# Decay table of a gated delta rule: differences and mask on GpSimd, one exponential per 16 rows and direction

## The chip, the cores and the metric

The kernel runs on one core of a Trainium2 chip. The metric is the device time of one execution in microseconds; the median of the runs counts. The engines are TensorE (PE in the profile, its weight loads PEld), VectorE (DVE), ScalarE (ACT), GpSimd (POOL) and SyncE (SP, which issues loads). Each engine works through its own instructions in a fixed order; semaphores tie the engines together.

## The reference, cut to what matters

One encoder layer over 512 tokens (two sequences of 256), width 2048: an RMS norm, one input projection, eight heads of neighbourhood attention beside eight heads of a gated delta rule that runs in both directions, an output projection, a SwiGLU, and a last norm. The change concerns the delta rule. Its per-token decay `g` is summed along each chunk of 64 tokens, and each pair of tokens of a chunk gets the decay between them:

```python
g = jnp.cumsum(g.reshape(B, n, CHUNK, H).transpose(0, 3, 1, 2), axis=-1)
tri = jnp.tril(jnp.ones((CHUNK, CHUNK), dtype=bool))
diff = g[..., :, None] - g[..., None, :]
decay = jnp.where(tri, jnp.exp(jnp.where(tri, diff, 0.0)), 0.0)
a_mat = jnp.where(strict, jnp.einsum('bhncd,bhnsd->bhncs', k_beta, k) * decay, 0.0)
qk = jnp.where(tri, jnp.einsum('bhncd,bhnsd->bhncs', q, k) * decay, 0.0)
```

`a_mat` is then inverted (a triangular solve), and a recurrence over the four chunks follows.

## The kernel before

A "lane" is one chunk of one head, sequence and direction: 4 x 8 x 2 x 2 = 128 lanes, one per partition. Lanes 0 to 63 (`half[0]`) run forwards, 64 to 127 (`half[1]`) backwards. The table of decays is `E`, 64 x 64 values per lane: `E[lane, s, c] = exp(G[c] - G[s])` for c >= s forwards and c <= s backwards, zero elsewhere. `G` is the running sum of `g`.

The projection is a long list of column tiles (`col_tile`): each is two halves (`half_gemm`), a half being 24 matmuls of 128x512 (three products of high and low parts for each of eight slices). The weights of a half are loaded by SP (`w_raw`) and split into `w_hi` (ACT, L139) and `w_lo` (DVE, L140); there are three buffers of each, so a half is split while PE works on one of the two before it. TensorE's order is pinned. Between matmuls `pump()` advances generators that put side work into the same queues.

First come the eight delta-rule heads: per head a k and a q tile. Each is scaled out of PSUM (`ev_xi`, DVE L308), convolved with five taps (`cacc`: one ACT instruction at L352, four DVE instructions at L358), and put through Silu (`kq`, ACT L362). The q tile is squared and split (`q_sq` L611, `sqh`, `sql`). `gates()` computes the gates and `G` beside head 0 (L456, L457). From head `DECAY_HEAD` = 2 on, `decays` adds that head's share of the exponentials right after `sqh` and `sql`, and their place in ACT's order is pinned. Some tiles later `kq_post` runs for the head: 16 small matmuls into two `ps_s` tiles (the Gram products), a third `ps_s` tile for sums of squares; ACT copies them out (`gs` L386, `qrow` L394), and GpSimd stores them (`s_gram` L388, `s_qq` L395; `s_kq` L623). The pool `psm` has three `ps_s` tiles in all, and `gs` has one buffer for each of the two sequences.

After head 7's Gram products are stored, `lanes()` begins: GpSimd loads all of them as `kkq` (L497), ACT copies the table to the other half of the partitions (L502), DVE multiplies it by `E` (L548, L556, L557), and then runs the triangular solve column by column (`prod` L578, `W` L580), beside the neighbourhood attention's projection (`qT` L709, `kT` L714). The recurrence, the output projection and the SwiGLU follow.

A scheduler orders the instructions of DVE, ACT and GpSimd by its own estimate of when they are ready, except where the source pins them.

Of the kernel before, what the change touches and what calls it, by code (L numbers as in the profile page):

```python
# [8 lines left out]
F32 = mybir.dt.float32  # L9
# [3 lines left out]
AF = mybir.ActivationFunctionType  # L13
ALU = mybir.AluOpType
# [4 lines left out]
P = 128  # L19
# [6 lines left out]
C = 64  # L26
# [38 lines left out]

ROW_FACTORS = 24
DECAY_HEAD = 2
DECAY_ROWS = 11


def r32(ap):
# [4 lines left out]
def hybrid_encoder(ctx: ExitStack, tc: tile.TileContext, xT, w_in, w_ba, w_out, w_gate,  # L76
                   w_up, w_down, w_group, nw_mix, nw_ffn, nw_fin, na_bias, conv_w, lane_par,
                   dn_nw, y):
    nc = tc.nc
    act = nc.scalar.activation  # L80
    tt = nc.vector.tensor_tensor
    ts = nc.vector.tensor_scalar
    stt = nc.vector.scalar_tensor_tensor

    pin = tc.keep_in_program_order
# [50 lines left out]
    def split(hi, lo, src, scale=None):  # L136

        if scale is None:
            act(out=hi, in_=src, func=AF.Copy)  # L139
            tt(lo, src, r32(hi), ALU.subtract)  # L140
        else:
            act(out=hi, in_=src, func=AF.Copy, scale=scale)
            stt(lo, src, scale, r32(hi), ALU.mult, ALU.subtract)
# [31 lines left out]
    def advance(queue):  # L175
        while queue:
            try:
                next(queue[0])
                return
            except StopIteration:  # L180
                queue.pop(0)
# [19 lines left out]
    def pause(n):  # L201
        for _ in range(n):
            yield
# [11 lines left out]
    def col_tile(src, xs):  # L215
        ps = pg.tile([P, T], F32, tag="g", name="ps_g")
        half_gemm(ps, src[0], xs[:8], True, False)
        half_gemm(ps, src[1], xs[8:], False, True)
        return ps
# [121 lines left out]
    half = (slice(0, 64), slice(64, 128))  # L341
# [6 lines left out]
    def conv_silu(ps, ct, out):  # L348

        xi = evac(ps, "xi", 2)  # L350
        ac = wk.tile([P, T], F32, tag="cacc", bufs=1, name="cacc")
        act(out=ac, in_=xi, func=AF.Copy, scale=cw[:, ct, 2:3])  # L352
        x3 = xi.rearrange("p (b t) -> p b t", b=NB)
        a3 = ac.rearrange("p (b t) -> p b t", b=NB)
        for j in (0, 1, 3, 4):
            o = j - 2
            lo, hi = max(0, -o), L - max(0, o)
            stt(a3[:, :, lo:hi], x3[:, :, lo + o:hi + o], cw[:, ct, j:j + 1], a3[:, :, lo:hi],  # L358
                ALU.mult, ALU.add)
        o5 = out.rearrange("p (b q c t) -> p b q c t", b=NB, q=2, c=2)  # L360
        for pp in range(2):
            pin(act(out=o5[:, :, pp], in_=ranged(ac, pp), func=AF.Silu))  # L362
# [39 lines left out]
    ln = ln_cm.__enter__()  # L402
# [7 lines left out]
    def vec(nm, w=C):  # L410
        return ln.tile([P, w], F32, tag=nm, name=nm)

    gt = {}

    def gates():
        bl, al = vec("bl", 4 * C), vec("al", 4 * C)
        for d in range(2):
            for t, r in ((bl, d * 8), (al, 16 + d * 8)):
                for k in range(4):
                    p0 = d * 64 + k * 16  # L420
                    nc.gpsimd.dma_start(
                        t[p0:p0 + 16].rearrange("p (g t) -> p g t", g=4),
                        s_ba[:, r:r + 8].rearrange("g h (b c t) -> (h b) g c t", b=NB, c=4)[:, :, k])
        yield from pause(GATE_START)
        for t in (bl, al):
            pin(tt(t[:, :2 * C], t[:, :2 * C], t[:, 2 * C:], ALU.add))
            pin(tt(t[:, :C], t[:, :C], t[:, C:2 * C], ALU.add))
        bl, al = bl[:, :C], al[:, :C]

        xa, ax, e, z, z2, sp = vec("xa"), vec("ax"), vec("e"), vec("z"), vec("z2"), vec("sp")  # L430
        pin(ts(xa, al, lpar[:, 0:1], None, ALU.add))
        act(out=ax, in_=xa, func=AF.Abs)
        act(out=e, in_=ax, func=AF.Exp, scale=-1.0)
        ea = vec("ea", 1)
        act(out=ea, in_=lpar[:, 1:2], func=AF.Exp)
        yield
        pin(ts(z, e, 2.0, None, ALU.add))
        pin(nc.vector.reciprocal(z, z))
        pin(tt(z, z, e, ALU.mult))
        pin(tt(z2, z, z, ALU.mult))  # L440
        pin(ts(sp, z2, 1.0 / 17, 1.0 / 15, ALU.mult, ALU.add))
        for n in (13, 11, 9, 7, 5, 3, 1):
            if n % 4 == 1:
                yield
            pin(tt(sp, sp, z2, ALU.mult))
            pin(ts(sp, sp, 1.0 / n, None, ALU.add))
        yield
        pin(stt(sp, sp, 2.0, z, ALU.mult, ALU.mult))
        pin(stt(sp, xa, 0.0, sp, ALU.max, ALU.add))
        g = vec("g")  # L450
        pin(ts(g, sp, ea, -1.0, ALU.mult, ALU.mult))

        on = vec("on")
        nc.vector.memset(on, 1.0)
        G, NG = vec("G"), vec("NG")
        nc.vector.tensor_tensor_scan(G[half[0]], on[half[0]], g[half[0]], 0.0, ALU.mult, ALU.add)  # L456
        nc.vector.tensor_tensor_scan(G[half[1], ::-1], on[half[1]], g[half[1], ::-1], 0.0,  # L457
                                     ALU.mult, ALU.add)
        ts(NG, G, -1.0, None, ALU.mult)
        tot = vec("tot", 1)  # L460
        nc.vector.tensor_copy(tot[half[0]], G[half[0], C - 1:C])
        nc.vector.tensor_copy(tot[half[1]], G[half[1], 0:1])

        yield
        beta = vec("beta")
        act(out=beta, in_=bl, func=AF.Exp, scale=-1.0)
        ts(beta, beta, 1.0, None, ALU.add)
        nc.vector.reciprocal(beta, beta)

        kd, eg, el = vec("kd", 2 * C), vec("eg"), vec("el", 1)  # L470
        act(out=kd[:, :C], in_=G, func=AF.Exp, scale=-1.0, bias=tot)
        act(out=eg, in_=G, func=AF.Exp)
        act(out=el, in_=tot, func=AF.Exp)
        nc.vector.tensor_copy(kd[:, C:], kd[:, :C])
        dg = vec("dg", P)
        ts(dg, ident, el, None, ALU.mult)
        E = ln.tile([P, C, C], F32, tag="E", name="E")
        nc.gpsimd.memset(E, 0.0)
        gt.update(G=G, NG=NG, beta=beta, kd=kd, eg=eg, dg=dg, E=E)

    def decays(s0, s1):

        G, NG, E = gt["G"], gt["NG"], gt["E"]
        for s in range(s0, s1):
            pin(act(out=E[half[0], s, s:], in_=G[half[0], s:], func=AF.Exp,  # L485
                    bias=NG[half[0], s:s + 1]))
            pin(act(out=E[half[1], s, :s + 1], in_=G[half[1], :s + 1], func=AF.Exp,  # L487
                    bias=NG[half[1], s:s + 1]))

    def lanes():  # L490
        beta, kd, eg, dg, E = (gt[n] for n in ("beta", "kd", "eg", "dg", "E"))
# [112 lines left out]
    for h in range(H):  # L604
        kq = wk.tile([P, 2, T], F32, tag="kq", bufs=2, name="kq")
        ps = (ps_k0, ps_k1)[h] if h < 2 else col_tile(w_in[2 * h], xs)
        conv_silu(ps, 8 + h, kq[:, 0])
        ps = (ps_q0, ps_q1)[h] if h < 2 else col_tile(w_in[2 * h + 1], xs)
        conv_silu(ps, h, kq[:, 1])
        sq = na.tile([P, T], F32, tag="qT", name="q_sq")  # L610
        pin(act(out=sq, in_=kq[:, 1], func=AF.Square))  # L611
        sqh = na.tile([P, T], F32R, tag="s0", name="sqh")
        sql = na.tile([P, T], F32R, tag="s1", name="sql")
        split(sqh, sql, sq)
        if h == 0:
            side.append(gates())
            advance(side)
        if h >= DECAY_HEAD:
            while side:
                advance(side)  # L620
            s0 = (h - DECAY_HEAD) * DECAY_ROWS
            decays(s0, min(C, s0 + DECAY_ROWS))
        nc.gpsimd.dma_start(s_kq[h], kq)  # L623
        chains.append(kq_post(h, kq, sqh, sql))

# [812 lines left out]
```

## Time and profile before

| | |
|---|---|
| median of 3 runs | 2275.26 us (2273.75 to 2276.0) |
| the profiled execution's own time | 2273.82 us |
| its span | 2272.0 us |
| busy: PE, DVE, ACT, POOL | 99%, 78%, 47%, 10% |
| granted TensorE clock | 0.998 |
| delta-rule heads | about 0 to 216 us |
| start of `lanes()` to the end of its solve | about 223 to 480 us |

The span runs from the first instruction of the program to the end of the last. Busy PE says that matmuls are in flight, not that they flow at their best; what TensorE waited for, and when, is in the waits by engine. In a timeline, a row is one instruction or several merged ones (x2), with its start, its time, and in brackets the idle time of the engine before it and what ended that.

### The profile page before, as it was taken

Reading aid. Unit: us, or ns where it says so; the run is one execution under the profiler, and the core shown is the slowest. Engines: PE = TensorE matmul, PEld = TensorE weight load, DVE = VectorE, ACT = ScalarE, POOL = GpSimd, SP = SyncE. Lnnn points to the kernel's source line nnn. Section 1 sums busy time; section 2 is a strip of 40 time slices with the busy share of each in tenths; the row PEclk is TensorE's granted clock in tenths of the full one; section 3 lists DMA queues with packets and bytes.
Section 4 is the critical chain, followed back from the end, with each engine's and each line's share of the span. In section 5 each row is a group of like instructions: output and inputs, shape, how many; then the busy total and the mean of one; then the engine's idle time right before and its main releaser. Section 6 shows DMA issues by size and latency. Waiting matters only on the chain.

```text
span 2272.0 us, 32550 instructions
## 1 busy us (share of the span) xinstructions
PE 2242.9 (99%) x12306; PEld 1918.1 (84%) x12306; DVE 1765.7 (78%) x2713; ACT 1065.2 (47%) x1670; POOL 236.9 (10%) x343
## 2 busy tenths in 40 slices
PE   9999999999999999999999999999999999999998
PEld 7787778888888888888888888888888878888887
DVE  7754699974556546898888888888888788998966
ACT  6777332333433425644444444444444454444435
POOL 1221100010000010110111110101100011011010
PEclk9999999999999999999999999999999999999999
DMA  5343422354333555777777777777777477667672
GB/s 212 113 137 133 122 94 96 103 132 143 103 103 103 186 176 172 218 200 206 203 198 203 193 206 203 212 200 205 201 198 190 148 201 202 174 190 210 183 201 87
DMA packets 113117, 383.96 MB, mean 169 GB/s; under 512 B 14112, under 2 KB 14448, under 8 KB 112704
## 3 DMA queue, kind: packets, MB, share of 16 engines
q1 hardware_dynamic: 77552, 267.17, 34.6%
q0 software_dynamic: 34256, 112.61, 23.5%
q8 instruction: 97, 1.59, 0.3%
q10 hardware_dynamic: 1152, 2.10, 0.3%
q14 instruction: 60, 0.49, 0.1%
HBM read 346.41 MB, written 35.41 MB: 168 GB/s over the span
## 4 chain that ended last, share of the span: by engine, by line
PE 83%; DVE 7%; ACT 5%; DMA 3%; issue 2%; SPq 0%; POOL 0%; DVEq 0%; ACTq 0%; POOLq 0%
PE ps_g L88 27%; PE ps_d L88 14%; PE ps_c L88 14%; PE ps_a L88 14%; PE ps_b L88 7%; PE ps_s L88 6%; DVE w_lo L140 2%; DVE cacc L358 1%; ACT w_hi L139 1%; DVE prod L578 1%; DMA w_first<-in_w_group_dram 1%; DMA w_raw<-in_w_in_dram 1%; ACT E L485 1%; DVE W L580 1%; ACT E L487 1%
## 5 line engine op out<-in xcount | busy, mean ns | idle before, releaser
L88 PE MATMUL ps_g<-xhi,w_hi 128*128 128x512 f32 x880 | 352.2, 400 | 1.0 <-ACT w_hi L139 1.0
L88 PE MATMUL ps_g<-xhi,w_lo 128*128 128x512 f32 x880 | 344.5, 392 | 2.1 <-DVE w_lo L140 2.0
L88 PE MATMUL ps_g<-xlo,w_hi 128*128 128x512 f32 x880 | 343.6, 391 | 0.5 <-DVE xlo L258 0.5
L140 DVE TENSOR_TENSOR w_lo<-w_raw,w_hi 128x1024 fp32r<-128x1024 f32 x164 | 200.2, 1221 | 140.4 <-ACT w_hi L139 138.7
L139 ACT ACTIVATE w_hi<-b 128x1024 fp32r<-128x1024 f32 (+1 forms) x180 | 185.8, 1032 | 237.0 <-issue 119.4
L139 ACT ACTIVATE w_hi<-w_raw 128x1024 fp32r<-128x1024 f32 x164 | 172.6, 1057 | 241.9 <-PE ps_g L88 188.8
L139 ACT ACTIVATE w_hi<-w_first 128x1024 fp32r<-128x1024 f32 (+1 forms) x180 | 185.4, 1030 | 185.9 <-PE ps_c L88 90.2
L140 DVE TENSOR_TENSOR w_lo<-w_first,w_hi 128x1024 fp32r<-128x1024 f32 (+1 forms) x180 | 213.7, 1187 | 65.2 <-ACT w_hi L139 61.7
L140 DVE TENSOR_TENSOR w_lo<-b,w_hi 128x1024 fp32r<-128x1024 f32 (+1 forms) x180 | 213.0, 1183 | 7.5 <-ACT w_hi L139 7.0
L88 PEld LDWEIGHTS ps_g<-xhi,w_lo 128*128 128x128 f32 x880 | 165.3, 188 | 40.0 <-DVE w_lo L140 4.8
L88 PEld LDWEIGHTS ps_g<-xhi,w_hi 128*128 128x128 f32 x880 | 165.5, 188 | 37.1 <-issue 2.6
L88 PEld LDWEIGHTS ps_g<-xlo,w_hi 128*128 128x128 f32 x880 | 165.6, 188 | 33.5 <-DVE xlo L258 1.2
L88 PE MATMUL ps_d<-xc,w_hi 128*128 128x512 f32 x704 | 175.2, 391 | 0.0
L88 PE MATMUL ps_c<-xc,w_hi 128*128 128x512 f32 x704 | 175.2, 391 | 0.0
L88 PE MATMUL ps_a<-xc,w_hi 128*128 128x512 f32 x696 | 173.1, 391 | 0.0
L88 PEld LDWEIGHTS ps_c<-xc,w_hi 128*128 128x128 f32 x704 | 129.5, 188 | 24.9
L88 PEld LDWEIGHTS ps_d<-xc,w_hi 128*128 128x128 f32 x704 | 129.4, 188 | 24.9
L88 PEld LDWEIGHTS ps_a<-xc,w_hi 128*128 128x128 f32 x696 | 128.1, 188 | 24.7
L139 ACT ACTIVATE w_hi<-w_second 128x1024 fp32r<-128x1024 f32 (+1 forms) x60 | 62.0, 1034 | 97.9 <-DVE ga L1134 45.0
L88 PE MATMUL ps_d<-xc,w_lo 128*128 128x256 f32 x704 | 98.6, 283 | 0.0
L88 PE MATMUL ps_c<-xc,w_lo 128*128 128x256 f32 x704 | 98.6, 283 | 0.0
L88 PE MATMUL ps_a<-xc,w_lo 128*128 128x256 f32 x696 | 97.5, 283 | 0.0
(381 smaller groups left out, 4231.9 us busy)
## 6 DMA issues: line engine op xcount, KB each, us to landing
w_raw<-in_w_in_dram SPq DMA_DIRECT2D x108, 512.0 KB, 3.3
b<-in_w_gate_dram SPq DMA_DIRECT2D x66, 512.0 KB, 4.2
b<-in_w_up_dram SPq DMA_DIRECT2D x66, 512.0 KB, 4.9
b<-in_w_group_dram SPq DMA_DIRECT2D x48, 448.0 KB, 4.1
w_raw<-in_w_out_dram SPq DMA_DIRECT2D x32, 512.0 KB, 3.4
w_raw<-in_w_down_dram SPq DMA_DIRECT2D x24, 512.0 KB, 4.0
w_second<-in_w_gate_dram SPq DMA_DIRECT2D x22, 512.0 KB, 7.0
w_first<-in_w_gate_dram SPq DMA_DIRECT2D x22, 512.0 KB, 4.5
```

The costliest lines, as they stand in the source:

```text
L88: pin(nc.tensor.matmul(*a, **k))
L139: act(out=hi, in_=src, func=AF.Copy)
L140: tt(lo, src, r32(hi), ALU.subtract)
L358: stt(a3[:, :, lo:hi], x3[:, :, lo + o:hi + o], cw[:, ct, j:j + 1], a3[:, :, lo:hi], ALU.mult, ALU.add)
L485: pin(act(out=E[half[0], s, s:], in_=G[half[0], s:], func=AF.Exp, bias=NG[half[0], s:s + 1]))
L487: pin(act(out=E[half[1], s, :s + 1], in_=G[half[1], :s + 1], func=AF.Exp, bias=NG[half[1], s:s + 1]))
L578: stt(pv, W[:, s0:s1, s0:c], ndm[:, c:c + 1], kkq[:, c, 0, None, s0:c].broadcast_to([P, n, j]), ALU.mult, ALU.mult)
L580: nc.vector.tensor_reduce(W[:, s0:s1, c], pv, AX.X, ALU.add)
```

## The change

`decays` no longer issues one exponential per row s and direction, 22 rows-and-directions per head over six heads. It works on 16 rows at a time (`Q` = 16), for heads 2 to 5 only. For each of the two directions GpSimd subtracts `G[s]` from `G[c]` for the 16 rows and all columns from the block's first (forwards) or up to its last (backwards): 16 x 64, 48, 32 or 16 values per lane, straight into `E`. A third GpSimd instruction adds `far` to the 16 x 16 block on the diagonal; `far` holds 0 in the triangle that is wanted and -1e30 in the other, so that the exponential gives zero there. Then one exponential per direction works on the whole block in place. `far` is written once, in `gates()`, by 31 memsets on GpSimd. The negated sum `NG` is gone.

```diff
-DECAY_ROWS = 11
+Q = 16
...
-        ts(NG, G, -1.0, None, ALU.mult)
...
+        far = ln.tile([P, Q, Q], F32, tag="far", name="far")
+        nc.gpsimd.memset(far, 0.0)
+        for s in range(Q):
+            if s:
+                nc.gpsimd.memset(far[half[0], s, :s], -1e30)
+            if s < Q - 1:
+                nc.gpsimd.memset(far[half[1], s, s + 1:], -1e30)
...
-    def decays(s0, s1):
-        G, NG, E = gt["G"], gt["NG"], gt["E"]
-        for s in range(s0, s1):
-            pin(act(out=E[half[0], s, s:], in_=G[half[0], s:], func=AF.Exp,
-                    bias=NG[half[0], s:s + 1]))
-            pin(act(out=E[half[1], s, :s + 1], in_=G[half[1], :s + 1], func=AF.Exp,
-                    bias=NG[half[1], s:s + 1]))
+    def decays(q):
+        G, E, far = gt["G"], gt["E"], gt["far"]
+        sl = slice(q * Q, q * Q + Q)
+        blocks = [E[half[0], sl, q * Q:], E[half[1], sl, :q * Q + Q]]
+        for hf, to in enumerate((G[half[0], q * Q:], G[half[1], :q * Q + Q])):
+            shape = [C, Q, to.shape[1]]
+            nc.gpsimd.tensor_tensor(blocks[hf], to[:, None].broadcast_to(shape),
+                                    G[half[hf], sl, None].broadcast_to(shape), op=ALU.subtract)
+        nc.gpsimd.tensor_tensor(E[:, sl, sl], E[:, sl, sl], far, op=ALU.add)
+        for b in blocks:
+            pin(act(out=b, in_=b, func=AF.Exp))
...
-        if h >= DECAY_HEAD:
+        if 0 <= h - DECAY_HEAD < C // Q:
             while side:
                 advance(side)
-            s0 = (h - DECAY_HEAD) * DECAY_ROWS
-            decays(s0, min(C, s0 + DECAY_ROWS))
+            decays(h - DECAY_HEAD)
```

TensorE's instructions and their order are the same. Three places show how the others move.

First ScalarE, from the end of head 2's exponentials on. Before, the last four of the 22 and what follows them:

```order
L485 ACTIVATE E<-G,NG 64x55
L487 ACTIVATE E<-G,NG 64x10
L485 ACTIVATE E<-G,NG 64x54
L487 ACTIVATE E<-G,NG 64x11
L362 ACT_TABLE_LOAD
L362 ACTIVATE kq<-cacc 128x2x128 x2
L386 COPY gs<-ps_s 128x256 x2
L394 COPY qrow<-ps_s 1x2x2x64
L394 COPY qrow<-ps_s 1x2x128
L139 ACTIVATE w_hi<-w_raw 128x1024
```

And now, from head 2's `sqh` on:

```order
L139 ACTIVATE sqh<-q_sq 128x512
L498 ACT_TABLE_LOAD
L498 ACTIVATE E<-E 64x1024
L498 ACTIVATE E<-E 64x16x16
L386 COPY gs<-ps_s 128x256
L139 ACTIVATE w_hi<-w_raw 128x1024
L362 ACT_TABLE_LOAD
L362 ACTIVATE kq<-cacc 128x2x128 x2
L386 COPY gs<-ps_s 128x256
L394 COPY qrow<-ps_s 1x2x2x64
L394 COPY qrow<-ps_s 1x2x128
```

Two exponentials stand where 22 stood. Of head 1's two `gs` copies the first now comes right behind them, the second behind a weight split and head 3's Silu of k (`kq`), which needs DVE's convolution.

Second GpSimd, from the stores of head 0's Gram products on. Before:

```order
L623 DMA s_kq<-kq 128x1024 x2
L388 DMA s_gram<-gs 64x2x128 x4
L395 DMA s_qq<-qrow 2x4x64
L623 DMA s_kq<-kq 128x1024
L388 DMA s_gram<-gs 64x2x128 x4
L395 DMA s_qq<-qrow 2x4x64
```

And now the same stretch, as far as the second quarter's mask:

```order
L632 DMA s_kq<-kq 128x1024 x2
L388 DMA s_gram<-gs 64x2x128 x2
L494 TENSOR_TENSOR E<-G 64x1024
L494 TENSOR_TENSOR E<-G 64x16x16
L388 DMA s_gram<-gs 64x2x128
L496 TENSOR_TENSOR E<-E,far 128x16x16
L388 DMA s_gram<-gs 64x2x128
L494 TENSOR_TENSOR E<-G 64x16x48
L395 DMA s_qq<-qrow 2x4x64
L494 TENSOR_TENSOR E<-G 64x16x32 x2
L496 TENSOR_TENSOR E<-E,far 128x16x16
```

All twelve subtractions and masks, those of heads 3 to 5 too, stand here in one run; head 2's `s_kq` and the stores of head 1 come behind the last of them.

Third ScalarE again, from head 7's `sqh` to the copies of `kkq`. Before, the last exponentials and what follows:

```order
L485 ACTIVATE E<-G,NG 64x1
L487 ACTIVATE E<-G,NG 64x64
L139 ACTIVATE w_hi<-w_raw 128x1024
L386 COPY gs<-ps_s 128x256 x2
L394 COPY qrow<-ps_s 1x2x2x64
L394 COPY qrow<-ps_s 1x2x128
L139 ACTIVATE w_hi<-w_raw 128x1024 x2
L502 COPY kkq<-kkq 64x2048 x2
```

And now:

```order
L139 ACTIVATE sqh<-q_sq 128x512
L139 ACTIVATE w_hi<-w_raw 128x1024
L386 COPY gs<-ps_s 128x256 x2
L394 COPY qrow<-ps_s 1x2x2x64
L394 COPY qrow<-ps_s 1x2x128
L139 ACTIVATE w_hi<-w_raw 128x1024 x2
L512 COPY kkq<-kkq 64x2048 x2
```

Head 7's `gs` copies no longer stand behind that head's share of exponentials (18 of them).

More of the change, by code (lines that the diff above doesn't have):

```diff
@@ L454, in gates @@
         nc.vector.memset(on, 1.0)
-        G, NG = vec("G"), vec("NG")
+        G = vec("G")
         nc.vector.tensor_tensor_scan(G[half[0]], on[half[0]], g[half[0]], 0.0, ALU.mult, ALU.add)
@@ L478, in gates @@
         nc.gpsimd.memset(E, 0.0)
-        gt.update(G=G, NG=NG, beta=beta, kd=kd, eg=eg, dg=dg, E=E)
-    def decays(s0, s1):
-        G, NG, E = gt["G"], gt["NG"], gt["E"]
-        for s in range(s0, s1):
-            pin(act(out=E[half[0], s, s:], in_=G[half[0], s:], func=AF.Exp,
-                    bias=NG[half[0], s:s + 1]))
-            pin(act(out=E[half[1], s, :s + 1], in_=G[half[1], :s + 1], func=AF.Exp,
-                    bias=NG[half[1], s:s + 1]))
+        far = ln.tile([P, Q, Q], F32, tag="far", name="far")
[5 more added lines that the diff above has]
+                nc.gpsimd.memset(far[half[1], s, s + 1:], -1e30)
+        gt.update(G=G, far=far, beta=beta, kd=kd, eg=eg, dg=dg, E=E)
+    def decays(q):
[9 more added lines that the diff above has]
+            pin(act(out=b, in_=b, func=AF.Exp))
     def lanes():
```

## The prediction

> **What bounds the kernel now.** The page's first part names the engine, the waits of TensorE say what it waited for in the stretch that the change can reach (80 to 300 us), and the windows cut that stretch into pieces.
>
> ```profile
> PE 2242.9 (99%) x12306; PEld 1918.1 (84%) x12306; DVE 1765.7 (78%) x2713; ACT 1065.2 (47%) x1670; POOL 236.9 (10%) x343
> ```
>
> ```profile
> engine line waited for: us in total, times, longest us
> PE ps_s L88 <- DVE kT L714: 2.2, 1, 2.2
> PE ps_s L88 <- ACT gs L386: 1.5, 1, 1.5
> PE ps_g L88 <- DVE w_lo L140: 1.4, 3, 0.6
> PE ps_g L88 <- ACT w_hi L139: 0.8, 1, 0.8
> PE ps_s L88 <- ACT sqh L139: 0.4, 1, 0.4
> PE ps_s L88 <- DVE sql L140: 0.3, 1, 0.3
> ```
>
> ```profile
> 114.00:170.00 56.00, 55.85 (x281) 44.97 (x280) 30.05 (x38) 44.64 (x99) 11.07 (x19) 1.00 0.43 138
> 170.00:227.00 57.00, 56.24 (x273) 45.31 (x272) 27.50 (x32) 43.94 (x98) 10.55 (x19) 1.00 0.39 131
> 227.00:284.00 57.00, 53.27 (x244) 43.39 (x243) 37.24 (x83) 20.96 (x31) 5.98 (x15) 1.00 0.44 123
> ```
>
> The columns of a window are PE, PEld, DVE, ACT and POOL busy, then the clock. TensorE is the bound, and its work does not change. ACT is busy 79% of the heads (44.64 of 56), but TensorE stands still there only 0.15 us in one window and 0.76 in the next. So 37 us taken from ACT are not 37 us of time: the gain can be no more than the waits listed, 6.6 us, plus a little that counts as issue. 0.2% of this kernel, about what a measurement can tell from no change, is 4.55 us.
>
> **ScalarE.**
>
> ```profile
> L485 ACT ACTIVATE E<-G,NG x64: 294/322/349, 101.6 to 221.2; 64x64 f32<-64x64 f32 x1, 64x63 f32<-64x63 f32 x1, 64x62 f32<-64x62 f32 x1, 64x61 f32<-64x61 f32 x1
> L487 ACT ACTIVATE E<-G,NG x64: 289/317/345, 102.0 to 221.5; 64x1 f32<-64x1 f32 x1, 64x2 f32<-64x2 f32 x1, 64x3 f32<-64x3 f32 x1, 64x4 f32<-64x4 f32 x1
> ```
>
> ```profile
> 95.66 1.28 ACT L362 ACT_TABLE_LOAD   x1 [3.74 <-DVE cacc L358]
> 97.58 1.04 ACT L139 ACTIVATE w_hi<-w_raw 128x1024 fp32r<-128x1024 f32 x1
> 99.66 0.61 ACT L139 ACTIVATE sqh<-q_sq 128x512 fp32r<-128x512 f32 x1
> 100.30 1.28 ACT L485 ACT_TABLE_LOAD   x1
> ...
> 110.82 0.63 ACT L386 COPY gs<-ps_s 128x256 f32<-128x256 f32 x2
> 111.86 1.05 ACT L139 ACTIVATE w_hi<-w_raw 128x1024 fp32r<-128x1024 f32 x1
> ```
>
> Removed: 64 x 0.322 + 64 x 0.317 = 40.9 us, whatever their width. Added: eight exponentials over 1024, 768, 512 and 256 values per lane, twice each. None is in the trace; ACT's 128x1024 took 1.05 us and its 128x256 copies 0.63 for two, so about 1.05, 0.83, 0.58 and 0.35, twice: 5.6 us (between 2.8, all like the smallest, and 8.4, all like the largest). Two loads of tables at 1.28 go as well: 38 us less on ACT. What of it reaches TensorE are three waits in the heads: head 1's `gs` copies stand behind 22 exponentials until 110.82, and TensorE, whose three `ps_s` tiles all belong to head 1 until then, waits 1.5 us with head 2's Gram products; and 0.4 and 0.3 us on `sqh` and `sql`. Together 2.2 us.
>
> **The start of the lanes.**
>
> ```profile
> 214.32 1.09 PE L88 MATMUL ps_s<-kq 128*64 128x128 f32 x16
> ```
>
> ```profile
> 222.81 0.63 ACT L386 COPY gs<-ps_s 128x256 f32<-128x256 f32 x2
> 236.76 1.90 ACT L502 COPY kkq<-kkq 64x2048 f32<-64x2048 f32 x1 [10.38 <-DMA kkq<-s_gram]
> 246.68 1.91 ACT L502 COPY kkq<-kkq 64x2048 f32<-64x2048 f32 x1
> 248.61 1.06 ACT L139 ACTIVATE w_hi<-w_raw 128x1024 fp32r<-128x1024 f32 x1
> ```
>
> Head 7's Gram products were done at 215.4, yet its copies came at 222.81, behind head 7's exponentials and a weight split. There are none for head 7 now, so store, load and copies of `kkq` begin 5 to 7 us sooner against TensorE's work. Before, a 1.9 us copy stood right ahead of the weight split of 248.61; the waits on `w_hi` 0.8, `w_lo` 1.4 and `kT` 2.2 (behind the first products with `E` and the solve) all lie in this stretch, 4.4 us. How much goes depends on where the copies fall between the splits: from nothing to 4.4. I take 4, near the top, since 5 to 7 us are more than any one of these waits.
>
> **GpSimd.**
>
> ```profile
> 0.74 0.20 POOL masks.py:197 MEMSET ident<- 128x128 f32 x1 [0.29 <-POOLq L1424]
> 2.11 0.33 POOL masks.py:199 TENSOR_SCALAR_AFFINE_SELECT ident<-ident 128x128 f32<-128x128 f32 x1
> 38.91 3.54 POOL L478 MEMSET E<- 128x4096 f32 x1 [34.36 <-ACT x_sq L298]
> 54.75 2.06 POOL L421 DMA_DIRECT2D bl<-s_ba  x4 [1.31 <-issue]
> ...
> 87.67 1.19 POOL L388 DMA_DIRECT2D s_gram<-gs  x2 [0.36 <-ACT gs L386]
> 97.97 0.57 POOL L623 DMA_DIRECT2D s_kq<-kq  x1 [7.07 <-ACT kq L362]
> 111.46 2.42 POOL L388 DMA_DIRECT2D s_gram<-gs  x4 [12.92 <-ACT gs L386]
> ```
>
> The 31 memsets of `far` stand ahead of the loads `bl` and `al`. Next to 0.20 us for 128 values they are at most 0.2 each, 6 us, likelier half; 1.3 us of that was idle anyway. The four groups of four such loads were issued by 54.75 + 4 x 2.06 = 63, and DVE first adds `bl` at 70.51, so I cost them at nothing; without that cover they would delay `G`, which nobody needs before 100.3.
>
> ```profile
> 70.51 0.29 DVE L426 TENSOR_TENSOR bl<-bl 128x128 f32<-128x128 f32 x1
> 87.69 0.29 DVE L457 TENSOR_TENSOR_SCAN G<-on,g 64x64 f32<-64x64 f32 x1
> 88.01 0.69 DVE L140 TENSOR_TENSOR sql<-q_sq,sqh 128x512 fp32r<-128x512 f32 x1
> 91.34 1.23 DVE L140 TENSOR_TENSOR w_lo<-w_raw,w_hi 128x1024 fp32r<-128x1024 f32 x1 [0.18 <-ACT w_hi L139]
> 92.48 3.10 DVE L358 SCALAR_TENSOR_TENSOR cacc<-ev_xi,cw,cacc 128x508 f32<-128x508 f32 x4
> 98.66 1.23 DVE L140 TENSOR_TENSOR w_lo<-w_raw,w_hi 128x1024 fp32r<-128x1024 f32 x1 [3.08 <-ACT w_hi L139]
> ...
> 101.06 2.31 DVE L358 SCALAR_TENSOR_TENSOR cacc<-ev_xi,cw,cacc 128x510 f32<-128x510 f32 x3
> ```
>
> The twelve `tensor_tensor` treat 2 x 16 x (64+48+32+16) + 4 x 256 = 6144 values per lane, from 88 us on, when `G` is there. No such instruction is in the trace. From below: a memset writes 4096 values in 3.54 us, 0.86 ns each; with 0.1 us per instruction 6.5 us. From above: reading one operand made the 128-wide select 0.13 us longer than the memset, 1.0 ns a value; two operands and a write make 2.9 ns, 19 us. They do read two, so nearer to that: 15 us, 1.25 us each on average.
>
> The Trainium skill (GPSIMD Engine Reference, Performance versus the Vector engine) gives 4497 ns for 2048 values of a two-input add on GpSimd; an estimate from that page would be 13.5 us, and 1.5 less in the sum below.
>
> What does this cost? Two bounds. If GpSimd works beside the others, nothing: the first quarter's three instructions end by 93 or so and ACT asks at 101.6; the store behind the run moves from 97.97 to 105, and the next ones are only due at 111.46. If GpSimd and DVE take turns wherever both read two operands from SBUF, DVE's chain is stretched. From 88 to 95.6 that is `sql`, `w_lo` and four `cacc`, six instructions; each may find one of GpSimd's 1.25 us under way, 7.5 us, less what falls into DVE's gaps: 6. Head 2's last `cacc` ends at 101.6, and ACT, which had been idle 3.74 us for it before, gets to `sqh` at 106 instead of 99.7, and through 1.28 + 1.05 + 0.35 us of table and exponentials to the first `gs` at 109. The second `gs` now stands behind head 3's Silu, whose `cacc` chain has met five more turns: about 115.5. TensorE needs both tiles from 109.5 on: a stall of 6 us where 1.5 was. Queued behind ACT's copies, and behind DVE's turns, are the next weight splits; at 115.5 they are no later than the 111.86 of before by more than the two halves (5.4 us each, 24 matmuls) that are split ahead. GpSimd ends at 88 + 15 + some 9 (DVE's instructions above: 0.69 + 1.23 + 3.10 + 1.23 + 2.31 = 8.6) = 112, and head 1's stores, which free `gs` for head 2, are issued by 116.
>
> The trace cannot tell the two apart; it shows only that a GpSimd instruction that writes does not hold DVE up: beside the memset of 38.91 a `w_lo` took 1.23 us, as at 91.34.
>
> ```profile
> 40.64 1.23 DVE L140 TENSOR_TENSOR w_lo<-w_raw,w_hi 128x1024 fp32r<-128x1024 f32 x1
> ```
>
> The Trainium skill (SBUF — State Buffer, Who interferes with whom) says that a DVE instruction with two SBUF inputs and a GpSimd instruction that reads SBUF exclude each other for the whole instruction, and that one which only writes does not; the row above agrees with the second half, and no run here shows the first. By that rule the turns are taken and the change gains next to nothing; without it the first rival below holds.
>
> I take the turns as likelier, since both engines are dense there: 5.0 of DVE's 7.6 us from 88 to 95.6 are such instructions.
>
> The rest is small: `NG` (one DVE instruction) goes; on SP one weight load moves ahead of a prefetch of `kq`; DVE's order in the solve swaps neighbours.
>
> **Sum**, against the profiled execution's 2273.8 us: - 2.2 (waits in the heads) - 4 (lanes) + 6 (new stall) = - 0.2, 2273.6. The median of the runs lies 1.4 above that execution: 2275.0.
>
> **Rivals.**
> *Free running*: GpSimd's work costs TensorE nothing. Sum - 6.2, median 2269, faster. For it: GpSimd was busy 10%, and the run lies ahead of need. Against it: two engines reading the same memory side by side for 20 us is not in this trace.
> *A slow GpSimd*: turns are taken and the twelve cost 23 us instead of 15, above my upper row, because operands repeated across rows or columns are read dearer than a plain one. Each further us on GpSimd lengthens the same chain by nearly as much, first through DVE's turns, then through head 1's stores, which head 2's `gs` copies on ACT need. Sum + 8, median 2283, slower. It decides from some 20 us on. For it: a select of only 128 values took 0.33 us. Against it: 0.86 ns per value for a memset leaves room.
> Turns and slow instructions would show at 88 to 120 us and nowhere else.
>
> **The numbers.** Turns at 15 us, no change within 0.2%: 0.41, its own range 2271 to 2279.5 (a stall of 2.5 to 10 us with the two bounds on GpSimd). Free running: 0.28, faster. Slow GpSimd: 0.31, slower. The forecast is the likeliest, 2275. The range reaches down through the free run, 2267.5, and up to the middle of the slow case, 2284; outside lie some 0.05 below and 0.12 above.
>
> **What would show it.** Right: `cacc` and `w_lo` stretched from 0.78 and 1.23 us between 88 and 113, GpSimd's twelve through by about 112, TensorE waiting 5 to 6 us on `gs` near 110, and the waits on `kT`, `w_hi` and `w_lo` of 240 to 300 mostly gone. Free running: `cacc` as before, no wait at 110. Slow: GpSimd at work past 118, ACT waiting at `gs` for stores. Wrong altogether: the stall elsewhere, or the lanes no better, which takes away 4 us of the gain.

## The result, and the profile after

The changed kernel takes 2268.68 us in the median (8 runs, 2267.16 to 2270.67), the kernel before 2274.83 (8 runs beside them); the ratio is 0.9972 with a 95% interval of 0.9961 to 0.9982. It is faster by 6.15 us, 0.28%, so the forecast of no change fell. The time lies inside the range, but only because the range reaches down through the rival of free running: the forecast's own part of it began at 2271. The profiled execution after took 2269.94 us, its span is 2268.1, 3.9 us shorter than the one before.

The engine totals of the page after, then the waits of TensorE from 80 to 300 us, then its windows:

```profile
PE 2242.2 (99%) x12306; PEld 1919.1 (85%) x12306; DVE 1773.0 (78%) x2712; ACT 1030.6 (45%) x1548; POOL 255.7 (11%) x386
```

```profile
PE ps_s L88 <- ACT gs L386: 2.2, 1, 2.2
```

```profile
114.00:170.00 56.00, 56.00 (x279) 44.67 (x276) 32.55 (x39) 36.44 (x58) 12.23 (x22) 0.97 0.43 136
...
227.00:284.00 57.00, 57.00 (x265) 47.69 (x264) 43.05 (x111) 27.25 (x46) 3.44 (x10) 1.00 0.42 122
```

ACT does 34.6 us less (38 in the prediction). Of the six groups of waits before, one is left, on `gs`, now 2.2 us long; the lane start is free of waits (57.00 us busy of 57, where 53.27 stood). The clock in the first window is 0.97, not 1.00.

TensorE's work and order are unchanged, so one can compare when it reaches the same instruction. Four of them, in the timeline of before (head 7's Gram products, the third, stand in the prediction at 214.32) and of after: the norm's sum of squares, head 3's Gram products, head 7's, and the first product with `dg` beside the solve.

```profile
45.65 1.02 PE L88 MATMUL ps_s<-ssq_acc,ones 128*128 128x512 f32 x2
...
123.74 1.09 PE L88 MATMUL ps_s<-kq 128*64 128x128 f32 x16
...
360.98 0.38 PE L88 MATMUL ps_s<-dg,ones 128*128 128x128 f32 x2
```

```profile
46.60 0.59 PE L88 MATMUL ps_s<-ssq_acc,ones 128*128 128x512 f32 x1
...
127.02 1.09 PE L88 MATMUL ps_s<-kq 128*64 128x128 f32 x16
...
215.95 1.09 PE L88 MATMUL ps_s<-kq 128*64 128x128 f32 x16
...
355.44 0.38 PE L88 MATMUL ps_s<-dg,ones 128*128 128x128 f32 x2
```

The differences of the starts give the three stretches that the change can reach: early heads (to head 3), late heads (3 to 7), and lanes. Worked out in the same way from every trace below (one trace of each kernel):

| kernel | early heads | late heads | lanes | median us |
|---|---|---|---|---|
| before | 78.09 | 90.58 | 146.66 | 2274.83 |
| after | 80.42 | 88.93 | 139.49 | 2268.68 |
| 13 rows a head | 82.17 | 94.00 | 141.44 | 2276.38 |
| twelve on DVE | 76.46 | 88.93 | 139.58 | 2265.21 |
| from head 4 | 76.46 | 88.93 | 139.56 | 2265.08 |
| none | 76.47 | 88.92 | 140.01 | 2265.27 |
| 18 behind head 7 | 76.46 | 88.93 | 140.02 | 2267.15 |
| spread | 76.46 | 88.93 | 140.48 | 2265.90 |
| twice | 87.35 | 88.93 | 140.14 | 2276.47 |
| only writes | 76.46 | 88.93 | 140.65 | 2264.89 (one run) |
| 36 behind head 7 | 76.46 | 88.93 | 145.20 | 2269.83 |

After against before: + 2.33, - 1.65, - 7.17, together - 6.49. The rest of the two profiled executions (0.95 us later at the first of the four, + 1.64 after the last) makes - 3.9 of it. It lies outside these stretches, and what comes after them varies by 3.2 us between the traces of the table (1910.9 to 1914.1 us); the medians, 6.15 apart, are close to the sum of the three.

### The profile page after: what moved, and what is told of

Same layout as the page of the kernel before. It is cut to its first block, busy times and chain, and to the rows that moved or that the text cites. A ratio compares the mean times of both kernels' runs of the same rounds, so it can differ in the third digit from the quotient of the medians.

```text
span 2268.1 us, 32470 instructions
## 1 busy us (share of the span) xinstructions
PE 2242.2 (99%) x12306; PEld 1919.1 (85%) x12306; DVE 1773.0 (78%) x2712; ACT 1030.6 (45%) x1548; POOL 255.7 (11%) x386
## 4 chain that ended last, share of the span: by engine, by line
PE 92%; DVE 4%; ACT 1%; issue 1%; DMA 1%; SPq 0%; DVEq 0%; POOL 0%; ACTq 0%; POOLq 0%
PE ps_g L88 35%; PE ps_d L88 14%; PE ps_c L88 14%; PE ps_a L88 14%; PE ps_b L88 7%; PE ps_s L88 7%; DVE cacc L358 1%; DVE w_lo L140 1%; PE ps_s L91 1%; DMA w_first<-in_w_group_dram 1%; PE ps_o L88 1%; ACT w_hi L139 1%; ACT yo L877 0%; DMA x_raw<-in_xT_dram 0%; DMA w_second<-in_w_group_dram 0%
```

## The experiments

Each was timed in five rounds beside runs of the kernel before on the same chip (medians 2274.58 to 2275.20), the one with only writes once. The theory after the result: the gain is the waits of the lanes and of the heads, and the turns between GpSimd and DVE (one waits while the other reads) give back 3 to 4 us of it through one stall at head 2.

**What the lanes wait for: 13 rows a head, before's way.**

```diff
-DECAY_ROWS = 11
+DECAY_ROWS = 13
```

> The kernel before with 13 rows per head instead of 11: the same 128 exponentials on ACT, but in heads 2 to 6, none behind head 7. Theory (the gain at the lanes comes from head 7 having no exponentials, wherever the others stand): the waits on kT, w_lo and w_hi between 220 and 300 us, 4.4 us, go; in the heads four exponentials more per head (1.3 us) lengthen the wait on gs at 109 from 1.5 to about 2.8 and add two or three of 0.5 to 1 us; together 1 us faster than before, between 3 faster and the same. Rival (what pays is the 38 us less work on ACT, or the other order that the scheduler gives DVE in the solve): the three waits stay and the time is that of before or up to 3 us more.

Measured: 2276.38 us (2274.54 to 2278.16) against 2275.20; ratio 1.0004, interval 0.9995 to 1.0012. TensorE's waits from 80 to 300, and ACT around head 7:

```profile
PE ps_s L88 <- ACT gs L386: 3.5, 2, 2.8
PE ps_g L88 <- DVE w_lo L140: 1.1, 2, 0.5
...
```

```profile
222.56 0.63 ACT L139 ACTIVATE sqh<-q_sq 128x512 fp32r<-128x512 f32 x1
...
224.05 0.63 ACT L386 COPY gs<-ps_s 128x256 f32<-128x256 f32 x2
```

The wait on `kT` is gone, and those on the splits up to 300 now lie in the heads. The lanes are 5.2 us shorter with the same 128 exponentials on ACT, so it is not the amount of ACT's work that counts there. But the heads cost more than expected: 4.1 and 3.4 us, where I had put some 3.5 in all, and the whole comes out level (the interval holds 1).

**The turns: the twelve on DVE.**

```diff
-            nc.gpsimd.tensor_tensor(blocks[hf], ...
+            nc.vector.tensor_tensor(blocks[hf], ...
...
-        nc.gpsimd.tensor_tensor(E[:, sl, sl], E[:, sl, sl], far, op=ALU.add)
+        nc.vector.tensor_tensor(E[:, sl, sl], E[:, sl, sl], far, op=ALU.add)
```

> The changed kernel with its twelve tensor_tensor on DVE instead of GpSimd: GpSimd reads nothing beside DVE any more. Theory (the wait of 2.2 us on gs at 109 to 111 and the 3 us of half clock behind it come from turns between GpSimd and DVE): DVE's w_lo take 1.23 us again and four cacc 3.1; the wait and the half clock go; 3.6 us faster than the changed kernel, some 2265. Rival (the wait comes from the second gs standing behind head 3's Silu in ACT's order, turns or none): it stays at 1 to 2 us, 2268.5. Second rival (DVE itself is the bound there and twelve instructions of about 1 us more make its splits late): waits of TensorE on w_lo of 3 us or more between 90 and 115, 2271 or above.

Measured: 2265.21 us, ratio to before 0.9956 (0.9942 to 0.9969). DVE's and then ACT's timeline:

```profile
92.58 1.21 DVE L140 TENSOR_TENSOR w_lo<-w_raw,w_hi 128x1024 fp32r<-128x1024 f32 x1
...
101.72 1.22 DVE L494 TENSOR_TENSOR E<-G 64x1024 f32<-64x1024 f32 x1
```

```profile
100.21 0.35 ACT L386 COPY gs<-ps_s 128x256 f32<-128x256 f32 x1
...
106.01 0.35 ACT L386 COPY gs<-ps_s 128x256 f32<-128x256 f32 x1
```

The view shows no wait of TensorE from 80 to 300. DVE does the whole subtraction itself and is still in time: 1.22 us for 64x1024, where GpSimd took 1.90 and held DVE up besides. The early heads take 76.46 us instead of 80.42: the stall and what follows it cost 3.96 us, and by the medians 3.5 (the intervals of the two ratios overlap a little). But one edit moved two things: the scheduler also put the first `gs` ahead of head 2's `q_sq` and `sqh`, and the second ahead of head 3's Silu. So this run alone does not part the turns from ACT's order; the version "spread" below does.

**Where the exponentials stand: from head 4.**

```diff
-DECAY_HEAD = 2
+DECAY_HEAD = 4
```

> The changed kernel with DECAY_HEAD = 4: the four pairs of exponentials beside heads 4 to 7, GpSimd's run as early as in the changed kernel. Theory (the turns cost only through the exponentials of head 2, which put head 1's gs behind head 3's convolution): the cacc and w_lo between 88 and 107 are as long as in the changed kernel, but head 1's gs copies leave ACT by 105, no wait there; two exponentials of 0.35 to 0.75 us each ahead of head 7's gs cost the lanes nothing; 3.6 us faster than the changed kernel, 2265. Rival (the turns make DVE's splits and convolutions late by themselves): a wait of 2 us or so stays at 105 to 116, 2268.5. Second rival (any exponential behind head 7 brings the lane waits back): kT or w_lo wait again near 250, 2268 to 2270.

Measured: 2265.08 us, ratio 0.9955 (0.9943 to 0.9968).

```profile
94.14 5.47 DVE L358 SCALAR_TENSOR_TENSOR cacc<-ev_xi,cw,cacc 128x508 f32<-128x508 f32 x4
102.69 2.70 DVE L140 TENSOR_TENSOR w_lo<-w_raw,w_hi 128x1024 fp32r<-128x1024 f32 x1 [3.08 <-ACT w_hi L139]
```

```profile
103.69 0.61 ACT L139 ACTIVATE sqh<-q_sq 128x512 fp32r<-128x512 f32 x1
104.22 0.62 ACT L386 COPY gs<-ps_s 128x256 f32<-128x256 f32 x2
```

The turns are all there, in the same run on GpSimd, and cost nothing: without a table load and two exponentials in between, both `gs` copies follow `sqh` at 104.22, and TensorE waits for nothing. So the turns alone do not make the stall. It takes turns together with ACT's order around head 2's exponentials, in which the second `gs` stands behind head 3's Silu.

**The floor: none of it.** The calls of differences, mask and exponentials are left out of `decays`.

> The changed kernel without differences, mask and exponentials; the table stays zero. It is the floor that any placement of them can reach. Theory: no wait at 80 to 120 and none of the lane waits, 2264.5, and the version on DVE and the late one within 1 us of it. Rival (a part of the changed kernel's gain or loss lies elsewhere than in these instructions): 2267 or above, with the wait on gs still there.

Measured: 2265.27 us, ratio 0.9958 (0.9945 to 0.997). The two versions above stand at this floor, so placing this work better promises no more.

**The lanes again: a block of 18 behind head 7.** On top of the version on DVE:

```diff
...
+        if h == 7:
+            for _ in range(9):
+                for hf in half:
+                    pin(act(out=gt["scr"][hf], in_=gt["G"][hf], func=AF.Exp))
```

> The version with the twelve tensor_tensor on DVE, and after head 7's sqh eighteen exponentials more of 64 values per lane into a scratch tile that nobody reads: head 7 has its block of 5.8 us and a table load again, with everything else gone. Theory (the 4.4 us of waits at the lanes come from that block alone, through the later kkq): the waits on kT, w_hi and w_lo between 220 and 300 come back, 4 us slower than the version on DVE, 2269. Rival (the waits came as much from the order in which the scheduler put kkq's copies, the splits and the solve on ACT and DVE, which differs here): 0 to 1.5 us slower, 2265 to 2267, with one wait near 250 or 275 at most.

Measured: 2267.15 us, ratio 0.9964 (0.9952 to 0.9977). The lanes' waits did not come back: a single one, 0.4 us on `w_lo`, and 140.02 us in the stretch against 139.58. ACT there, then head 7's Gram products on TensorE:

```profile
206.41 0.63 ACT L139 ACTIVATE sqh<-q_sq 128x512 fp32r<-128x512 f32 x1
...
208.36 5.01 ACT L636 ACTIVATE scr<-G 64x64 f32<-64x64 f32 x18
...
214.36 0.63 ACT L386 COPY gs<-ps_s 128x256 f32<-128x256 f32 x2
```

```profile
211.72 1.09 PE L88 MATMUL ps_s<-kq 128*64 128x128 f32 x16
```

And head 7's `sqh` before the change:

```profile
213.90 0.63 ACT L139 ACTIVATE sqh<-q_sq 128x512 fp32r<-128x512 f32 x1
```

My theory, that the block by itself is the cause, fell. ACT reaches `sqh` 5.3 us before TensorE begins head 7's Gram products, and most of the block lies in that lead; before the change the lead was 0.4 us (213.90 against 214.32). The heads' own blocks had used the lead up. The median is 1.9 us above the version on DVE, with overlapping intervals; the stretches account for 0.4 of it, and the rest I could not locate.

**A block of 36**, to tell a lead that is used up from an order with slack:

```diff
-            for _ in range(9):
+            for _ in range(18):
```

> As the version with eighteen exponentials more behind head 7's sqh, but with thirty-six, 10 us. There ACT came to its block at 207.1, 5.6 us before head 7's Gram products were through, and the gs copies left at 214.4, only 1.1 us after their end; before the change the block began at 214.6, 1.3 us before that end, and gs left 6.9 us after it. Theory (what the lanes feel is how long after the Gram products gs leaves ACT, so the blocks of heads 2 to 6, which made ACT late, had their part in it): gs leaves some 6 us after the products, kkq's copies end near 243, and 3 to 4.4 us of waits on kT, w_hi and w_lo between 220 and 300 come back, 2269. Rival (the order on ACT and DVE after the change has the slack, however late gs is): no wait above 1 us there, 2266 to 2267.

Measured: 2269.83 us, ratio 0.9979 (0.997 to 0.9988). Waits of TensorE from 216 to 345, and ACT:

```profile
PE ps_s L88 <- DVE kT L728: 2.0, 1, 2.0
PE ps_g L88 <- DVE w_lo L140: 1.7, 3, 0.8
```

```profile
207.78 10.04 ACT L636 ACTIVATE scr<-G 64x64 f32<-64x64 f32 x36
...
218.81 0.63 ACT L386 COPY gs<-ps_s 128x256 f32<-128x256 f32 x2
```

`gs` leaves 6.6 us after the end of the Gram products (211.15 + 1.09), the waits are back, and the lanes take 145.20 us. The lanes follow how long after those products `gs` leaves: 139.5 to 140.7 us in the seven kernels where it leaves at once, 140.0 at 1.5 us after, 145.2 at 6.6 after, and before the change, at 7.4 after, 146.7. The 13 rows, at 1.1 us after, do not quite fit with 141.4: there ACT comes to `sqh` 0.7 us after the products have begun, and TensorE waits 0.6 us on `sqh` and `sql` right behind them and 0.8 on `w_lo` after 300; some 0.5 us stay open. (The expectation's 1.1 and 6.9 count from the end of the two sums of squares behind the products.)

**GpSimd's place: spread.** The twelve, and the stores of `kq`, kept in program order:

```diff
+            pin(nc.gpsimd.tensor_tensor(blocks[hf], ...
...
+        pin(nc.gpsimd.tensor_tensor(E[:, sl, sl], E[:, sl, sl], far, op=ALU.add))
...
+        pin(nc.gpsimd.dma_start(s_kq[h], kq))
```

> The changed kernel with the twelve GpSimd instructions and the stores of kq kept in program order: each quarter's three stand beside its own head, near 88, 109, 131 and 150 us, instead of all in one run from 88 to 107. Theory (the price of the turns is their sum on one chain of DVE): 3 or 4 us of turns before head 2's first gs become at most 2, the wait of 2.2 us and the half clock go; one wait of up to 0.7 may come near 140; 2.7 us faster than the changed kernel, 2266. Rival (any turn delays head 2's chain enough, and the later quarters add stalls of their own at 120 to 160): waits on gs in two or more heads, 2269 or above.

Measured: 2265.90 us, ratio 0.9964 (0.995 to 0.9978). ACT's two `gs` copies of head 1, then DVE near the second quarter:

```profile
104.09 0.37 ACT L386 COPY gs<-ps_s 128x256 f32<-128x256 f32 x1
...
107.49 0.35 ACT L386 COPY gs<-ps_s 128x256 f32<-128x256 f32 x1
```

```profile
109.03 4.35 DVE L358 SCALAR_TENSOR_TENSOR cacc<-ev_xi,cw,cacc 128x508 f32<-128x508 f32 x3 [2.22 <-ACT cacc L352]
```

The turns still happen (4.35 us for three `cacc`, 2.31 alone), but one quarter's worth fits into each head's slack: no wait in the heads. ACT's order here is that of the changed kernel: between the two copies stand a weight split, the table load and head 3's Silu, as there. Only the turns are fewer, and the second copy comes at 107.49 instead of 113.02. So with this order it is the turns that make the stall.

**A slow GpSimd: every subtraction twice.**

```diff
+            for _ in range(2):
...
```

> The changed kernel with each of the eight subtractions issued twice: GpSimd's run gets longer by its eight subtractions, some 12 us, and ends near 125 with turns. It puts the prediction's rival of a slow GpSimd to the test. Theory (each further us on GpSimd lengthens DVE's chain and head 1's stores by nearly as much): a wait of TensorE of 6 to 8 us on gs near 110 and one of 2 near 130, 7 to 8 us slower than the changed kernel and slower than before, some 2276. Rival (once GpSimd's run is past head 3's first cacc it meets gaps of DVE, and costs no more): 1 to 3 us slower than the changed kernel, 2270 to 2272.

Measured: 2276.47 us (2274.23 to 2278.32), ratio to before 1.0007 (0.9998 to 1.0016). The longest wait of TensorE (one other, 0.6 us on `gs`, comes just before it), and ACT's next `gs`:

```profile
PE ps_s L88 <- ACT qrow L394: 8.2, 1, 8.2
```

```profile
121.21 0.37 ACT L386 COPY gs<-ps_s 128x256 f32<-128x256 f32 x1 [0.28 <-DMA s_gram<-gs]
123.87 0.37 ACT L386 COPY gs<-ps_s 128x256 f32<-128x256 f32 x1 [2.29 <-DMA s_gram<-gs]
```

The early heads take 6.9 us more than after the change, for eight more subtractions: GpSimd's run, with the stores in it, lasts 31.0 us instead of 18.3, and head 3's `cacc`, ahead of the Silu and `qrow`, are stretched further. ACT's order differs as well: both `gs` now stand ahead of the Silu, and only `qrow` waits behind it. ACT waits longer for the stores too, as the rival had it (2.6 us for these two copies; 0.7 before the change and after it), but TensorE's long wait was over at 119.4, and none follows up to 300: the stores cost it nothing that the trace shows. The expected second wait near 130 did not come.

**Reads or writes.** Memsets of the same blocks, each written twice and kept in program order, in place of the twelve; differences and mask are left out:

```diff
-            nc.gpsimd.tensor_tensor(blocks[hf], ...
+            for _ in range(2):
+                pin(nc.gpsimd.memset(blocks[hf], -1.0))
...
```

> The changed kernel with memsets in place of the subtractions and of the mask's addition: GpSimd writes the same blocks of the table, twice each, and reads nothing; differences and mask are left out. The memsets are kept in program order with the stores of kq. Theory (turns come only where GpSimd reads): cacc beside them stays at 0.78 each (3.1 for four) and w_lo at 1.23, TensorE's wait on gs is gone, about 2264 to 2266. Rival (any GpSimd instruction on SBUF takes turns with a DVE instruction that reads two operands): cacc groups beside memsets of 0.9 us stretched by 0.5 us or more per instruction.

Measured: 2264.89 us (one run). GpSimd, then DVE:

```profile
108.70 2.11 POOL L495 MEMSET E<- 64x768 f32 x3
```

```profile
108.52 1.53 DVE L358 SCALAR_TENSOR_TENSOR cacc<-ev_xi,cw,cacc 128x508 f32<-128x508 f32 x2
109.96 1.22 DVE L140 TENSOR_TENSOR w_lo<-w_raw,w_hi 128x1024 fp32r<-128x1024 f32 x1
```

Beside writes, `cacc` and `w_lo` take their usual time. Of the two-operand instructions only those beside GpSimd's reads are stretched.

## Why the prediction was right and wrong

**The turns: right.** DVE after the change:

```profile
88.97 2.21 DVE L140 TENSOR_TENSOR sql<-q_sq,sqh 128x512 fp32r<-128x512 f32 x1
...
92.21 1.28 DVE L308 TENSOR_TENSOR ev_xi<-ps_g,rstd 128x512 f32<-128x512 f32 x2
93.42 2.75 DVE L140 TENSOR_TENSOR w_lo<-w_raw,w_hi 128x1024 fp32r<-128x1024 f32 x1
96.09 6.00 DVE L358 SCALAR_TENSOR_TENSOR cacc<-ev_xi,cw,cacc 128x508 f32<-128x508 f32 x4
...
106.31 1.23 DVE L358 SCALAR_TENSOR_TENSOR cacc<-ev_xi,cw,cacc 128x508 f32<-128x508 f32 x1
```

Against 0.69, 1.23 and 3.10 these are 1.52 + 1.52 + 2.90 = 5.9 us of waiting; the term said 6. That the sum agrees to a tenth is partly luck: it gave each of six instructions up to 1.25 us and took 1.5 off for gaps, but two waited 1.52 and the four `cacc` 0.7 each on average. `ev_xi`, whose one operand is in PSUM, kept its time, 1.28 for two. This is what the Trainium skill (SBUF — State Buffer, Who interferes with whom) states: DVE's two SBUF inputs and GpSimd's reads exclude each other for the whole instruction, writes do not. The runs now show both halves.

**The stall of 6 us: the term that was mis-sized.** ACT and GpSimd after the change:

```profile
102.16 1.28 ACT L362 ACT_TABLE_LOAD   x1 [8.17 <-DVE cacc L358]
...
109.62 0.37 ACT L386 COPY gs<-ps_s 128x256 f32<-128x256 f32 x1
...
113.02 0.35 ACT L386 COPY gs<-ps_s 128x256 f32<-128x256 f32 x1
```

```profile
88.70 2.95 POOL L494 TENSOR_TENSOR E<-G 64x1024 f32<-64x1024 f32 x2 [0.45 <-DVE G L456]
...
103.34 1.90 POOL L494 TENSOR_TENSOR E<-G 64x1024 f32<-64x1024 f32 x1
...
106.94 0.59 POOL L632 DMA_DIRECT2D s_kq<-kq  x1
```

The first `gs` came at 109.6 (109 foretold). The second came at 113.0 and ended at 113.4, not 115.5: "head 3's Silu, whose `cacc` chain has met five more turns" is the step that failed. GpSimd was through at 107, not 112, since the twelve took some 16 us with their own waiting in it, where I had added all of DVE's 8.6 us to 15. Nor was 15 right: the shortest times of the forms in these runs (1.90, 1.47, 1.04 and 0.61 us for 1024, 768, 512 and 256 values, twice each, and 0.71 for each of four masks) add up to some 13, nearer to the prediction's other estimate of 13.5. So head 3's chain met one turn (1.23 us at 106.31), and the stall was 2.2 us. This trace comes to the heads 0.95 us later; with that taken off, the second `gs` ended 3 us sooner than in the prediction's working, and some 0.7 us more fell away because TensorE ran the first eight of head 2's 16 Gram products as soon as the first `gs` had left. The half clock behind it, told below, added 1.7, and the two make most of the 3.96 us that the stall cost by the stretch.

**The lanes: right in place, too small.** All 4.4 us of waits went, as `gs` of head 7 leaves without delay, but the stretch is 7.17 us shorter; the term said 4. My 4.4 was an upper bound read from TensorE's matmuls up to 300 us. Before's waits from 216 to 500, with those of the weight loads, show what it left out:

```profile
PEld ps_g L88 <- DVE w_lo L140: 4.5, 6, 1.1
...
PEld ps_s L88 <- DVE kT L714: 2.6, 1, 2.6
...
PE ps_s L88 <- DVE kT L714: 2.2, 1, 2.2
PE ps_g L88 <- DVE w_lo L140: 2.0, 4, 0.7
...
PEld ps_g L88 <- ACT w_hi L139: 1.8, 2, 1.2
...
PE ps_g L88 <- ACT w_hi L139: 1.0, 2, 0.8
```

The matmuls' waits come to 5.2 us up to 500, those of the weight loads, which run beside matmuls, to 8.9 (8.4 of it inside the stretch); the 7.17 lie between. After the change no such wait of a matmul is left there, and 0.8 us of the weight loads'. The lanes' data also came sooner than foretold: the first copy of `kkq` on ACT began 22.4 us after head 7's Gram products did, and now begins 12.3 after, 10 us sooner instead of 5 to 7. The reason was only half told, too: head 7's block cost what it did because the blocks of heads 2 to 6 had used up ACT's lead.

**The heads: right in place, too small.** - 1.63 (early, by the versions without a stall) and - 1.65 us, 3.3 against 2.2 from the matmuls' waits alone; before the change the weight loads waited 3.8 us for the same three, `gs`, `sqh` and `sql`.

**The sum.** - 3.3 + 4.0 - 7.2 = - 6.5, where - 2.2 + 6 - 4 gave - 0.2. Free running was priced at 2269 and the median is 2268.7, but by accident: it asked for no stall and no stretched `cacc`. The slow GpSimd is half borne out. A longer run of GpSimd does lengthen the heads, through DVE's turns, but at about half the price: 12.7 us more of it made the early heads 6.9 us longer, where the rival had nearly 1 for 1, and the stores had no part that the trace shows. Its reason, dearer repeated operands, shows in no run: at their shortest a subtraction of 256 values per lane took 0.61 us and a mask, whose operands are plain, 0.71. Even with every subtraction twice that kernel is level with before, since the lanes gained more than foretold.

## What to carry to other kernels

Before moving work off a busy engine, look for the instruction behind which a consumer's data stand, and for the lead with which that engine comes to it: some 35 us less on ACT were worth at most 10 here, most of it at the two places where `gs` left too late. GpSimd is not free beside a dense stream of two-operand DVE instructions; in this kernel the same subtractions on DVE itself, in the order that the scheduler then chose, cost TensorE nothing, and so did leaving them on GpSimd and starting the exponentials two heads later (2265.2 and 2265.1 us, 3.5 below the changed kernel and at the floor). An upper bound on a gain needs the waits of the weight loads and the whole stretch that the late work reaches.

## What the runs showed of the hardware

A short stall can cost TensorE its clock afterwards. Windows of after, then of the run with 13 rows (columns as in the prediction):

```profile
114.00:117.00 3.00, 3.00 (x13) 1.94 (x10) 2.39 (x4) 2.27 (x6) 2.40 (x5) 0.53 0.52 167
```

```profile
114.00:117.00 3.00, 3.00 (x12) 1.90 (x9) 2.69 (x3) 2.28 (x5) 2.42 (x6) 0.50 0.61 120
```

After the stall of 2.2 us at 111 the matmuls start 427 ns apart instead of 227 for some 3 us (a window of 113.4 to 116.8 us has a granted clock of 0.50). From the stall's Gram products to head 3's after the change takes 16.43 us, before it 12.52 (starts 110.59 and 127.02, 111.22 and 123.74); 2.17 of the 3.91 is the stall, 1.7 the clock. A stall is counted here from the start of one matmul to the start of the next, less the usual 0.23 us; the profile's own wait, which goes by modelled ends, is up to 0.2 us shorter. In the eleven traces TensorE stood still for 2.0 us or longer 14 times, and 7 of these were followed by such a stretch (after 2.0, 2.0, 2.2, 2.2, 3.0, 3.0 and 8.2 us), none of the some 90 stalls of 0.8 to 2.0 us. The Trainium skill (TensorE: Matmul & The Clock Gate, Part 1: The HAM clock gate) has the rate halve after an idle window of about 3.4 us that runs freely; here stalls clearly shorter than that were enough. Which stalls of 2.0 to 2.4 us are hit stays open; no run varied the length of a stall by itself.
